# A two-layer attention encoder: x and the output on GpSimd's DMA queue, a norm weight spread by a one-row matmul, and a new order of the first work

## The chip, the core and the metric

The kernel runs on one core of a Trainium2 chip. The metric is the device time of one execution in microseconds (us). Five engines work side by side, each through its own list of instructions in order: TensorE (PE, with its weight loads as PEld), VectorE (DVE), ScalarE (ACT), GpSimd (POOL) and SyncE (SP), which only issues DMA transfers here. GpSimd can issue transfers too. Sixteen DMA engines carry them.

## What is computed

A sequence of 512 positions with 1024 features goes through two layers and a last norm. Cut to what matters:

```python
for l in range(2):
    h = rmsnorm(x, norm_g[l])
    proj = h @ w_in[l]                       # 1024 x 4096
    out_a = neighborhood_attention(...)      # 8 heads x 64, columns 0..2047 of proj
    out_b = diff_attention(...)              # 4 heads, two softmax maps each
    y = concat(out_a * silu(g_a), out_b * silu(g_b))
    x = x + y @ w_out[l]
return rmsnorm(x, final_g)
```

where `rmsnorm(x, g) = x * rsqrt(mean(x*x) + 1e-6) * g`.

## The kernel before, in words

The 512 rows of x are held as four tiles of 128 rows (t = 0 to 3), each loaded by two transfers of 64 rows (`x_load`, L428 to L432), on SyncE's queue. A matmul in full precision is made of three terms: each operand is split into a high part (fp32r) and the rest, and high x high, low x high and high x low are summed.

Weights come in units of 256 columns of `w_in`. `load_raw` (L79) loads half a unit (4 of 8 row chunks, 512 KB); a cast on ScalarE makes the high part `wh`, a subtraction on GpSimd or VectorE the low part `wl` (L99, L101). There are two raw buffers, so the next half is loaded when the low part of one is done.

The first unit's work (L450 to L503) is written out by hand, and `pinned` (L439) keeps each engine in the order in which the program was written. What stands there, in words:

- the first norm's 1024 weights are loaded as a 128 x 8 block `gcol` (L452) and spread over all partitions as `g_bc` by eight TensorE transposes and two copies (L465 to L469); `warm` fills TensorE with unneeded products ahead of and behind that;
- `norm_stat` (L215) squares and sums one tile of x on ScalarE (L218) and takes the inverse root on GpSimd (L210, L212); `norm_apply` (L221) scales the tile on VectorE (L228), transposes it on TensorE (L234) and splits it into `hTh` on ScalarE (L205) and `hTl` on VectorE (L206);
- the first unit (called w0 here, its halves w0-lo and w0-hi) is cast at L476 and L477; its low parts are made on GpSimd (L478) and VectorE (L480);
- for each tile t, `proj_tm` with `groups=True` (L257, L267) multiplies: 8 products hTh x wh, 8 hTl x wh, 8 hTh x wl. Then come the next tile's `norm_apply`, for t < 2 the second unit's casts (`conv1`), and the copy of the result (`vb0_evac`). The squares of tiles 2 and 3 stand in the program at t = 0.

After it, the position tables are written to memory by 16 transfers on SyncE's queue (`t5_skew`, L135), behind the two transfers that wrap `hTh` and `hTl` round (L239), which need the last tile. The rest of both layers is ordered by the framework's scheduler. At the end of the second layer (L586 to L604), each tile's last quarter is added, squared and summed; GpSimd makes the scale (L210, L212), ScalarE and VectorE scale the tile (L601, L602), and two transfers of 64 rows store it on SyncE's queue (L604).

## Time and profile before

| | |
|---|---|
| time of three runs | 631.53, 633.57, 634.60 us, median 633.57 |
| profiled execution, span from first to last instruction | 630.6 us, which is all that is known of its own time |
| TensorE busy | 591.7 us (94%), mean granted clock 0.981 |
| VectorE, ScalarE, GpSimd busy | 422.3, 324.6, 277.3 us |
| moved by DMA | 77.57 MB, 123 GB/s over the span |
| idle TensorE at the start (7.3 to 13.0 and 22.3 to 26.7 us) | 5.7 and 4.5 us |
| from the last product's end (619.5 us) to the end of the span | 11.1 us |

Busy times overlap between engines and do not add up to the span. A wait is shown in brackets behind the instruction that ended it, with what released it. In the rows that follow, a window's row gives the busy time of each engine in a stretch, the granted clock of TensorE (1.00 is 2.4 GHz), the mean busy share of the sixteen DMA engines, and the bytes per time that they moved.

### The profile page before, as it was taken

Reading aid. Unit: us, or ns where it says so; the run is one execution under the profiler, and the core shown is the slowest. Engines: PE = TensorE matmul, PEld = TensorE weight load, DVE = VectorE, ACT = ScalarE, POOL = GpSimd, SP = SyncE. Lnnn points to the kernel's source line nnn. Section 1 sums busy time; section 2 is a strip of 40 time slices with the busy share of each in tenths; the row PEclk is TensorE's granted clock in tenths of the full one; section 3 lists DMA queues with packets and bytes.
Section 4 is the critical chain, followed back from the end, with each engine's and each line's share of the span. In section 5 each row is a group of like instructions: output and inputs, shape, how many; then the busy total and the mean of one; then the engine's idle time right before and its main releaser. Section 6 shows DMA issues by size and latency. Waiting matters only on the chain.

```text
span 630.6 us, 10037 instructions
## 1 busy us (share of the span) xinstructions
PE 591.7 (94%) x3626; PEld 522.3 (83%) x3626; DVE 422.3 (67%) x907; ACT 324.6 (51%) x706; POOL 277.3 (44%) x232
## 2 busy tenths in 40 slices
PE   4799699999899999999999999999989999999992
PEld 3678597888799878889999898888879878889992
DVE  3552354997988868874564257798888968874542
ACT  3343353864766555744343455666567646654421
POOL 2341422444456747743143633344535665733111
PEclk9799899999999999999999999999999999999997
DMA  6566746552442454264454452342343444355204
GB/s 145 129 124 192 213 147 197 134 136 78 109 119 55 143 129 133 85 171 146 134 168 135 123 144 86 90 114 63 88 107 93 116 116 116 101 167 168 68 1 134
DMA packets 77448, 77.57 MB, mean 123 GB/s; under 512 B 9906, under 2 KB 71346, under 8 KB 76374
## 3 DMA queue, kind: packets, MB, share of 16 engines
q1 hardware_dynamic: 75926, 74.53, 41.7%
q0 software_dynamic: 1472, 2.40, 2.3%
q8 instruction: 29, 0.48, 0.3%
q14 instruction: 21, 0.17, 0.1%
HBM read 63.16 MB, written 9.37 MB: 115 GB/s over the span
## 4 chain that ended last, share of the span: by engine, by line
PE 58%; DMA 14%; DVE 10%; issue 5%; POOL 5%; SPq 5%; ACT 3%; POOLq 0%; ACTq 0%; DVEq 0%
PE pp L252 25%; PE pp L267 22%; DMA wraw<-in_w_in_dram 4%; DMA y<-in_x_dram 4%; SPq L135 3%; DVE ea L382 2%; POOL wl L101 2%; DMA yb_d<-tb_d 2%; POOL ba L179 2%; PE pv L338 2%; DVE kt L291 2%; DVE w4k L329 1%; PE pt L333 1%; PE st L316 1%; DMA rs_d<-rsb 1%
## 5 line engine op out<-in xcount | busy, mean ns | idle before, releaser
L101 POOL TENSOR_TENSOR wl<-wraw,wh 128x1024 fp32r<-128x1024 f32 x68 | 166.2, 2462 | 192.5 <-ACT wh L99 124.9
L99 ACT CAST wh<-wraw 128x1024 fp32r<-128x1024 f32 x78 | 78.8, 1046 | 72.2 <-DMA wraw<-in_w_in_dram 28.9
L252 PE MATMUL pp<-hTh,wh 128*128 128x512 f32 x384 | 103.4, 397 | 3.2 <-DVE kt L291 3.2
L252 PE MATMUL pp<-hTh,wl 128*128 128x512 f32 x384 | 106.3, 398 | 0.0
L252 PE MATMUL pp<-hTl,wh 128*128 128x512 f32 x384 | 104.5, 398 | 0.0
L252 PEld LDWEIGHTS pp<-hTh,wh 128*128 128x128 f32 x384 | 70.4, 188 | 17.7 <-issue 3.6
L252 PEld LDWEIGHTS pp<-hTh,wl 128*128 128x128 f32 x384 | 70.3, 189 | 14.5 <-issue 0.5
L252 PEld LDWEIGHTS pp<-hTl,wh 128*128 128x128 f32 x384 | 70.2, 188 | 13.9
L267 PE MATMUL pp<-wh,hTh 128*128 128x256 f32 x256 | 72.3, 302 | 7.7 <-ACT hTh L205 4.5
L267 PE MATMUL pp<-wh,yTh 128*128 128x256 f32 x256 | 72.4, 283 | 0.0
L267 PE MATMUL pp<-wl,yTh 128*128 128x256 f32 x256 | 72.3, 283 | 0.0
L267 PE MATMUL pp<-wh,yTl 128*128 128x256 f32 x256 | 71.9, 283 | 0.0
L267 PE MATMUL pp<-wh,hTl 128*128 128x256 f32 x256 | 70.3, 293 | 0.0
L206 DVE TENSOR_TENSOR ptl<-pt,pth 128x256 fp32r<-128x256 f32 (+1 forms) x96 | 48.2, 507 | 31.6 <-ACT pth L205 30.7
L267 PE MATMUL pp<-wl,hTh 128*128 128x256 f32 x256 | 68.9, 287 | 0.0
L205 ACT CAST pth<-pt 128x256 fp32r<-128x256 f32 (+1 forms) x96 | 42.0, 443 | 43.1 <-PE pt L333 29.3
L382 DVE TENSOR_SCALAR ea<-ea,rza 128x256 f32<-128x256 f32 x64 | 58.5, 914 | 1.8
L267 PEld LDWEIGHTS pp<-wh,hTh 128*128 128x128 f32 x256 | 49.3, 202 | 10.9 <-ACT hTh L205 5.0
L179 POOL TENSOR_TENSOR ba<-nmask,ya 128x256 f32<-128x256 f32 (+1 forms) x64 | 39.6, 650 | 32.3 <-DVE mna L376 18.5
L319 DVE CUSTOM_DVE_ANT_0 lt<-st,yb 128x512 f32<-128x512 f32 x64 | 43.5, 685 | 11.2 <-PE st L317 10.7
L267 PEld LDWEIGHTS pp<-wh,hTl 128*128 128x128 f32 x256 | 48.8, 199 | 0.8
L267 PEld LDWEIGHTS pp<-wh,yTh 128*128 128x128 f32 x256 | 49.1, 192 | 0.2
(111 smaller groups left out, 1141.0 us busy)
## 6 DMA issues: line engine op xcount, KB each, us to landing
wraw<-in_w_in_dram SPq DMA_DIRECT2D x32, 512.0 KB
wraw<-in_w_in_dram SPq DMA_DIRECT2D x64, 256.0 KB
kt<-kt SPq DMA_DIRECT2D x16, 512.0 KB
wraw<-in_w_out_dram SPq DMA_DIRECT2D x16, 512.0 KB
y<-in_x_dram SPq DMA_DIRECT2D x16, 256.0 KB
ya_d<-rp_d SPq DMA_DIRECT2D x32, 120.0 KB
ya<-ya_d SPq DMA_DIRECT2D x16, 240.0 KB
yb<-yb_d SPq DMA_DIRECT2D x8, 280.0 KB
```

Of the source, the lines that this page charges most:

```text
L99: A.copy(out=wh[:, ks, :], in_=r)
L101: eng.tensor_tensor(out=wl[:, ks, :], in0=r, in1=wh[:, ks, :].bitcast(F32), op=ALU.subtract)
L135: eng.dma_start(out=dst[:, i * C8:(i + 1) * C8, :], in_=bass.AP(tensor=src.tensor, offset=src.offset + base - step * r - C8 * b, ap=[[pitc ...
L179: G.tensor_tensor(out=ba[:, i0:i0 + n], in0=_view(nmask, i0 * C8, [[C8, n], [0, ROWS], [1, C8]]), in1=_view(y, w0, [[C8, n], [RPW, ROWS], ...
L205: A.copy(out=oh, in_=ps)
L206: V.tensor_tensor(out=ol, in0=ps, in1=oh.bitcast(F32), op=ALU.subtract)
L252: T.matmul(out=pp, lhsT=a[:, kc, cs], rhs=b[:, kc, c0:c0 + S], start=(n == 0), stop=(n == 3 * KC - 1))
L267: T.matmul(out=pp[:, 0:256], lhsT=a[kc][:, c0:c0 + P], rhs=b[:, kc, :], start=(n == 0), stop=(n == 3 * KC - 1))
L291: V.tensor_tensor(out=kl, in0=src, in1=kh.bitcast(F32), op=ALU.subtract)
L319: V.tensor_tensor_reduce(out=lt, in0=st, in1=yb[:, 48 - 16 * qt:560 - 16 * qt], scale=1.0, scalar=3e38, op0=ALU.add, op1=ALU.min, accum_ou ...
L338: T.matmul(out=pv[:, qp * 256:(qp + 1) * 256], lhsT=vt[:, kt, h % 2, vs, :], rhs=pp[:, kt, :], start=(n == 0), stop=(n == 11))
L382: V.tensor_scalar_mul(e, e, rz)
```

## The change

The loads of x at the start go to GpSimd's queue, and so do the stores of the output. The first norm's weights are loaded as one row of 1024, and a matmul of a row of 128 ones with it spreads the row over all partitions. In the hand-written part, the square of tile 1 now stands ahead of w0-hi's cast, and the squares of tiles 2 and 3 stand just ahead of their own tile's scaling. The 24 products of a tile are taken in another sequence: first the four row chunks of w0-lo with hTh and hTl, then those of w0-hi, then both with `wl`. Lines move down by two or three.

```diff
+    one_row = work.tile([1, P], F32, name="row", tag="th", bufs=2)
+    V.memset(one_row, 1.0)
...
         if groups:
-            seq = [(kc, terms[i]) for i in (0, 2, 1) for kc in order]
+            seq = [(kc, terms[i]) for h0, i in ((0, 0), (0, 2), (4, 0), (4, 2), (0, 1), (4, 1))
+                   for kc in range(h0, h0 + 4)]
...
-    def x_load(t):
+    def x_load(t, eng=nc.sync):
...
-            nc.sync.dma_start(out=xi[64 * i:64 * i + 64], in_=x_v[2 * t + i])
+            eng.dma_start(out=xi[64 * i:64 * i + 64], in_=x_v[2 * t + i])
...
-    gcol = const.tile([P, KC], F32, name="gcol")
-    nc.sync.dma_start(out=gcol, in_=norm_g[0].rearrange("(k p) -> p k", p=P))
-    xt = [x_load(0)]
+    g_row = w4.tile([1, D], F32, name="g_row", tag="w4k")
+    nc.sync.dma_start(out=g_row, in_=norm_g[0:1, :])
+    xt = [x_load(0, nc.gpsimd)]
     raws = [load_raw(W.seq[0], hf) for hf in range(2)]
-    xt += [x_load(t) for t in range(1, NB)]
+    xt += [x_load(t, nc.gpsimd) for t in range(1, NB)]
...
-        for j in range(4):
-            T.transpose(out=gp[:, j * P:(j + 1) * P], in_=_view(gcol, 4 * i + j, [[0, P]]), identity=ident)
+        T.matmul(out=gp, lhsT=one_row, rhs=g_row[:, i * S:(i + 1) * S], start=True, stop=True)
...
-    n0 = norm_stat(xt[0])
...
+    ns = [norm_stat(xt[0])]
     A.copy(out=w[0][:, lo, :], in_=raws[0])
+    G.tensor_tensor(out=w[1][:, lo, :], in0=raws[0], in1=w[0][:, lo, :].bitcast(F32), op=ALU.subtract)
+    norm_apply(0, xt[0], g_bc, *ns[0])
+    ns.append(norm_stat(xt[1]))
     A.copy(out=w[0][:, hi, :], in_=raws[1])
-    G.tensor_tensor(out=w[1][:, lo, :], in0=raws[0], in1=w[0][:, lo, :].bitcast(F32), op=ALU.subtract)
-    norm_apply(0, xt[0], g_bc, *n0)
...
-    ns = [n0, norm_stat(xt[1])]
     for t in range(NB):
         pp = proj_tm(w, 64 + t * P, kh, kl, groups=True)
-        if t == 0:
-            ns += [norm_stat(xt[2]), norm_stat(xt[3])]
         if t + 1 < NB:
+            if t:
+                ns.append(norm_stat(xt[t + 1]))
             norm_apply(t + 1, xt[t + 1], g_bc, *ns[t + 1])
...
-                            nc.sync.dma_start(out=out_v[2 * t + i], in_=xn[t][64 * i:64 * i + 64])
+                            nc.gpsimd.dma_start(out=out_v[2 * t + i], in_=xn[t][64 * i:64 * i + 64])
```

How the instructions then stand on the engines, at the three places of which the prediction speaks. First ScalarE in the hand-written start, before (y_113, y_120, y_123 and y_126 are tiles 0 to 3 of x, wraw_116 and wraw_118 the halves of w0, wraw_189 and wraw_192 those of the second unit):

```order
L218 ACTIVATE w4k_157,ss_158<-y_113 128x1024
L476 CAST wh_163<-wraw_116 128x1024
L477 CAST wh_163<-wraw_118 128x1024
L205 CAST hTh_129<-pt_170 128x4x128
L205 CAST hTh_129<-pt_177 128x4x128
L218 ACTIVATE w4k_197,ss_198<-y_120 128x1024
L218 ACTIVATE w4k_228,ss_229<-y_123 128x1024
L218 ACTIVATE w4k_234,ss_235<-y_126 128x1024
L205 CAST hTh_129<-pt_242 128x4x128
L205 CAST hTh_129<-pt_249 128x4x128
L99 CAST wh_195<-wraw_189 128x1024
L205 CAST v_185<-pp_203 128x2x128
```

And the same engine with the change (tiles 0 to 2 are y_115, y_122 and y_125, w0's halves wraw_118 and wraw_120, the second unit's first half wraw_191):

```order
L220 ACTIVATE w4k_155,ss_156<-y_115 128x1024
L478 CAST wh_153<-wraw_118 128x1024
L207 CAST hTh_131<-pt_165 128x4x128
L207 CAST hTh_131<-pt_172 128x4x128
L220 ACTIVATE w4k_179,ss_180<-y_122 128x1024
L482 CAST wh_153<-wraw_120 128x1024
L207 CAST hTh_131<-pt_226 128x4x128
L207 CAST hTh_131<-pt_233 128x4x128
L101 CAST wh_197<-wraw_191 128x1024
L207 CAST v_187<-pp_199 128x2x128
L220 ACTIVATE w4k_269,ss_270<-y_125 128x1024
L207 CAST hTh_131<-pt_277 128x4x128
```

The squares of tiles 2 and 3 stood ahead of tile 1's two `hTh` casts; now they stand behind the whole of the tile before. w0-hi's cast moved behind tile 1's square.

GpSimd in the same place, with the change (before, all four pairs L210 and L212 stood ahead of the two L101):

```order
L479 TENSOR_TENSOR wl_154<-wraw_118,wh_153 128x1024
L212 TENSOR_SCALAR ss_180<-ss_180 128x1
L214 TENSOR_TENSOR rs_183<-ss_180,nhalf_98 128x1
L103 TENSOR_TENSOR wl_198<-wraw_191,wh_197 128x1024
L212 TENSOR_SCALAR ss_270<-ss_270 128x1
L214 TENSOR_TENSOR rs_273<-ss_270,nhalf_98 128x1
L103 TENSOR_TENSOR wl_198<-wraw_194,wh_197 128x1024
L212 TENSOR_SCALAR ss_329<-ss_329 128x1
L214 TENSOR_TENSOR rs_332<-ss_329,nhalf_98 128x1
```

The scales of tiles 2 and 3 now each stand behind a low part of the second unit.

GpSimd at the end, with the change (xn_6308 holds tiles 0 and 1, xn_6309 tiles 2 and 3; the stores stood on SyncE before):

```order
L212 TENSOR_SCALAR ss_6695<-ss_6695 128x1
L214 TENSOR_TENSOR rs_6698<-ss_6695,nhalf_98 128x1
L606 DMA out_0_dram<-xn_6308 8x8x1024 x2
L212 TENSOR_SCALAR ss_6732<-ss_6732 128x1
L214 TENSOR_TENSOR rs_6735<-ss_6732,nhalf_98 128x1
L606 DMA out_0_dram<-xn_6308 8x8x1024 x2
L212 TENSOR_SCALAR ss_6769<-ss_6769 128x1
L214 TENSOR_TENSOR rs_6772<-ss_6769,nhalf_98 128x1
L212 TENSOR_SCALAR ss_6806<-ss_6806 128x1
L214 TENSOR_TENSOR rs_6809<-ss_6806,nhalf_98 128x1
L606 DMA out_0_dram<-xn_6309 8x8x1024 x4
```

The stores of tiles 2 and 3 stand together behind the last tile's scale.

## Rows read from the trace of the kernel before

**Rows 1.** The page: span, and the chain that ended last, by line.

```profile
span 630.6 us, 10037 instructions
...
PE pp L252 25%; PE pp L267 22%; DMA wraw<-in_w_in_dram 4%; DMA y<-in_x_dram 4%; SPq L135 3%; DVE ea L382 2%; POOL wl L101 2%; DMA yb_d<-tb_d 2%; POOL ba L179 2%; PE pv L338 2%; DVE kt L291 2%; DVE w4k L329 1%; PE pt L333 1%; PE st L316 1%; 
```

**Rows 2.** Windows at the start and one later; last come PEclk, DMA share, GB/s.

```profile
1.60:2.60 1.00, 1.00 (x5) 1.00 (x6) 0.00 (x0) 0.61 (x2) 0.00 (x0) 1.00 0.54 4
2.60:4.00 1.40, 1.40 (x8) 1.40 (x8) 0.00 (x0) 0.00 (x0) 0.00 (x0) 1.00 0.41 32
4.00:10.00 6.00, 3.32 (x21) 2.80 (x19) 1.38 (x2) 0.00 (x0) 0.00 (x0) 1.00 0.96 205
10.00:15.00 5.00, 1.11 (x4) 0.71 (x4) 2.81 (x2) 3.71 (x5) 3.50 (x3) 0.76 0.58 180
...
55.00:60.00 5.00, 5.00 (x23) 4.06 (x22) 0.54 (x1) 0.04 (x1) 0.00 (x0) 1.00 0.80 252
```

**Rows 3.** Timeline of ScalarE at the start: start us, us, instruction, idle before.

```profile
10.09 1.06 ACT L218 ACTIVATE w4k<-y 128x1024 f32<-128x1024 f32 x1 [7.87 <-DMA y<-in_x_dram]
...
11.14 1.03 ACT L476 CAST wh<-wraw 128x1024 fp32r<-128x1024 f32 x1
...
17.39 1.06 ACT L218 ACTIVATE w4k<-y 128x1024 f32<-128x1024 f32 x1
...
25.05 1.06 ACT L218 ACTIVATE w4k<-y 128x1024 f32<-128x1024 f32 x1 [3.07 <-DMA y<-in_x_dram]
...
26.11 1.05 ACT L205 CAST hTh<-pt 128x512 fp32r<-128x512 f32 x2
...
28.00 0.38 ACT L205 CAST v<-pp 128x256 fp32r<-128x256 f32 x1
```

**Rows 4.** Timelines of VectorE (first three) and GpSimd at the start.

```profile
12.19 3.51 DVE L228 SCALAR_TENSOR_TENSOR w4k<-y,rs,g_bc 128x512 f32<-128x512 f32 x2 [6.16 <-ACT wh L476]
...
18.14 1.22 DVE L480 TENSOR_TENSOR wl<-wraw,wh 128x1024 fp32r<-128x1024 f32 x1
20.08 1.42 DVE L228 SCALAR_TENSOR_TENSOR w4k<-y,rs,g_bc 128x512 f32<-128x512 f32 x2 [0.72 <-POOL rs L212]
...
12.25 2.91 POOL L478 TENSOR_TENSOR wl<-wraw,wh 128x1024 fp32r<-128x1024 f32 x1
...
28.18 2.38 POOL L101 TENSOR_TENSOR wl<-wraw,wh 128x1024 fp32r<-128x1024 f32 x1 [1.07 <-ACT wh L99]
```

**Rows 5.** Timeline of TensorE at the start.

```profile
16.53 2.25 PE L267 MATMUL pp<-wh,hTh 128*128 128x256 f32 x8
...
26.72 2.08 PE L267 MATMUL pp<-wh,hTh 128*128 128x256 f32 x8 [4.46 <-ACT hTh L205]
...
31.26 1.29 PE L234 MATMUL pt<-ident,w4k 128*128 128x128 f32 x8
...
38.58 0.75 PE L267 MATMUL pp<-wh,hTh 128*128 128x256 f32 x4
```

**Rows 6.** Windows at the end: columns as in rows 2.

```profile
615.30:620.00 4.70, 4.16 (x35) 3.95 (x33) 1.89 (x6) 1.79 (x5) 1.49 (x4) 1.00 0.51 150
...
625.00:629.30 4.30, 0.00 (x0) 0.00 (x0) 0.00 (x0) 0.00 (x0) 0.00 (x0) 0.50 0.44 142
629.30:630.60 1.30, 0.00 (x0) 0.00 (x0) 0.00 (x0) 0.00 (x0) 0.00 (x0) 0.50 0.00 0
```

**Rows 7.** Timeline of GpSimd at the end: its last scale.

```profile
621.35 0.55 POOL L212 TENSOR_TENSOR rs<-ss,nhalf 128x1 f32<-128x1 f32 x1
```

**Rows 8.** A 256 KB transfer on GpSimd's queue: its issue, two windows, all eight landings.

```profile
155.37 0.54 POOL L359 DMA_DIRECT2D rb<-rs_d  x1 [2.28 <-DMA rs_d<-rsb]
...
155.40:156.60 1.20, 1.20 (x9) 1.00 (x8) 0.00 (x0) 0.25 (x1) 0.51 (x1) 1.00 0.00 0
156.60:158.60 2.00, 2.00 (x12) 1.66 (x11) 1.18 (x2) 1.45 (x3) 0.00 (x0) 1.00 0.58 131
...
DMA to landing us min/median/max: 3.4/3.6/3.8
```

## The prediction

> **What bounds the kernel now.** I read the page's chain first: TensorE's two projection lines carry 47% of a span of 630.6 us, the loads of x 4% [rows 1]. The middle of the program keeps its order on every engine, so only the two ends can move: the first 39 us, where TensorE waits for data, and the last 15, where the output is stored. Whatever the start saves is handed on, since all that follows hangs on the fourth tile's product (38.58 [rows 5]). I take the ends apart by the windows and by each engine's timeline.
>
> *The start.* ScalarE waits 7.87 us for tile 0 of x, until 10.09 [rows 3]. From 1.6 to 2.6 the DMA engines are half busy with 4 GB/s, the 4-byte pieces of `gcol`; 32 GB/s follow until 4.0, then 205 at a share of 0.96 while x and w0 share one queue, then 180 at 0.58 once the loads of x are nearly alone [rows 2]. ScalarE's last wait for x, 3.07 us for tile 3, ends at 25.05; two casts of tile 1 stand behind it, and TensorE, idle for 4.46, starts tile 1's product at 26.72 [rows 3, 5].
>
> *The end.* From 615.3 to 629.3 the stores move 142 to 150 GB/s at a share of 0.44 to 0.51; 1.3 us without traffic close the span [rows 6]. So eight transfers of 256 KB are limited by their own rate, and half of the DMA engines stand idle all the while. The same mark, 0.58 at 180 GB/s, is on the loads of x.
>
> **The weight row.** Two matmuls of 512 columns and two copies replace eight transposes and the same copies, before tile 0 arrives. The cover is TensorE's wait for its first product at 16.53; without it they would cost some 2 us, the 2.25 of eight products at the lower clock level [rows 5]. I take 0. The removed `gcol` frees up to 1.0 us of the DMA engines ahead of x.
>
> **x on GpSimd's queue.** On that queue bytes follow the issue by 1.2 us, and 256 KB are there 3.4 to 3.8 after it [rows 8]. Tile 0 is issued behind two memsets, the other six transfers behind the identity, each issue 0.54, so all eight are out by 6 us, beside w0 on SyncE's queue. I let tile 0's bytes start at 2.4 (2.6 now, less a little for `gcol`), keep the slow 1.4 us (to 3.8), and add 1.0 for the landing (nearest row: the tail of 1.3 [rows 6]). The rate of both queues together lies between 205 and 252 GB/s [rows 2]; I take 225, nearer the row at the same place, with 130 for x and 95 for w0, an even split leaning to x's longer rows. Tile 0's 0.52 MB then take 4.0: it lands at **8.8**; w0-lo 5.5, at 10.3; w0-hi at 15.8; the last of x at 18.8. Bounds for tile 0: 205 halved, landing 9.9; nearly all of 252, landing 7.0.
>
> **The new order of the first work.** What follows tile 0 is counted from its landing, X.
>
> - Now the scaling of tile 1 (20.08) starts 10.0 behind X [rows 3, 4].
> - With the change, tile 0's scaling still runs against GpSimd's `wl` (3.51 for a pair that takes 1.42 alone, beside 2.91 of GpSimd [rows 4]), so `hTh` of tile 0 ends where it does now and tile 1's square follows at X + 7.4 (17.39 - 10.09 [rows 3]). Behind it now stand w0-hi's cast, 1.03 [rows 3], and `wl` of w0-hi on VectorE, 1.22 [rows 4], ahead of tile 1's scaling: 7.4 + 1.25 (the square, 1.06, with its read) + 1.03 + 1.22 and hand-overs = **X + 11.0**. The new order costs 1.0 here: that cast lay in ScalarE's idle time.
> - From tile 1's scaling to tile 3's product it is 38.58 - 20.08 = 18.5 now [rows 4, 5], with the 3.07 wait inside. The change removes that wait, but the squares of tiles 2 and 3 come late. Counted from tile 1's scaling: tile 0's product ends at 2.6 (16 of its 24 products wait for w0-hi's cast); transposes, 1.29 [rows 5], and two casts end at 5.0, a weight cast at 6.0, the copy of v, 0.38, and tile 2's square at 7.7. GpSimd first makes 2.38 of `wl` [rows 4], until 8.4, then two small steps (0.55 for the larger [rows 7]) until 9.1; scaling, transposes and casts until 11.8. Then weight cast, tables (taken like a cast), v and square, 1.03 + 1.03 + 0.38 + 1.25, until 15.5; small steps until 16.3; half a scaling, 0.7, half the transposes, 0.65, and one cast, 0.6, until 18.3. I take 18.6 with hand-overs: the order puts back the wait that it removed.
>
> Start: 10.1 + 10.0 + 18.5 = 38.6 now; then 8.8 + 11.0 + 18.6 = 38.4, a gain of **0.2**. Its sign hangs on X (zero at 9.0): X = 9.9 loses 0.9, X = 7.0 gains 2.0.
>
> **The stores on GpSimd's queue.** GpSimd's scale for tile 3 ends at 621.9 [rows 7]; behind it stand the four stores of tiles 2 and 3, 0.54 each [rows 8], out by 624.1. Tile 2's, which go out before that scale now, wait for it. First bytes at 621.9 + 1.2 = 623.1. These 1.05 MB are bounded from both sides: at 150 GB/s 7.0 us (end of traffic 630.1), at 300, both halves of a tile on different DMA engines, 3.5 (626.6). I take 3.9 (627.0), near the fast end, since a share of 0.51 [rows 6] leaves eight engines idle and another queue's transfers need not go to the busy eight. With the tail of 1.3: 628.3 for 630.6, a gain of **2.3**. Bounds: gain 2.7, loss 0.8. Tile 1's stores also slip, by a square; they are out before tile 2's and cost nothing.
>
> *A rule against it.* The Trainium skill's DMA: Bandwidth & Descriptors, section Issuing engines are not separate DMA queues, says that transfers run on the same sixteen engines whoever issues them, and that spreading them over issuers saves issue time only. By it the end would lose the 0.8; the share of 0.51 in rows 6 shows engines that the stores leave unused, which that reading does not foresee.
>
> **Sum.** 0.2 + 2.3 = 2.5 of the profiled 630.6 gives 628.1; the median of the runs lies 2.97 above that span, so 633.57 - 2.5 = **631.1**.
>
> **Rivals.**
>
> 1. *The stores stay at half rate* (chance 0.2). GpSimd's transfers go to the same eight engines, or its queue moves no more than the 131 GB/s of rows 8 (then 8.0 us, 1.0 more). For it: that row. Against it: that transfer reads one 2 KB row 128 times, unlike a store. The end loses 0.8 instead of gaining 2.3: 633.57 - 0.2 + 0.8 = 634.2.
> 2. *x crowds out w0: slower* (chance 0.22). If each DMA engine takes turns by rows, 4 KB of x against 1 KB of w0, then w0-lo's 0.52 MB are through only with all 2.1 MB of x: at the 205 of rows 2, 3.8 + 12.8 + 1.0 = 17.6. Cast, two casts of `hTh`, square, w0-hi's cast and its `wl` (1.03 + 1.05 + 1.25 + 1.03 + 1.22 = 5.6) put tile 1's scaling at 23.2, 3.1 later than now, and tile 3's product 3.2 later. With the end's 2.3: 633.57 + 3.2 - 2.3 = 634.5; with rival 1's end 637.6. It decides where w0-lo lands after 14.4, or w0-hi after 17.5. For it: x is issued on a queue of its own and no longer waits its turn behind w0. Against it: w0 now goes out as SyncE's second and third transfers, ahead of most of x.
> 3. *Both loads fit* (chance 0.16). At 252 GB/s tile 0 comes nearly alone, at 7.0, and w0 still in time (both 3.15 MB are through by 17.3): start 2.0, end 2.7, so 628.9.
>
> **How the numbers follow.** My case has 0.42. The range takes in the rivals' 628.9 and 634.5 and the spread of three runs, 1.5 either way: 627.8 to 636.0. A measurement of this kernel tells about 0.5%, 3.2 us, from no change. Faster than 630.4: rival 3 and the better part of my case (0.16 + 0.2), 0.36. Slower than 636.7: rivals 1 and 2 together, 0.07. Between: 0.57.
>
> **What would show it.** Tile 0: its square starts near 8.8, and the DMA share of the first 15 us stays near 1. Order: tile 1's scaling comes 11 behind the first square's start, ScalarE waits for no later tile of x, GpSimd's small steps stand right behind a `wl`, and tile 3's product starts at 38.4. Stores: a share near 1 and 250 to 300 GB/s from 623 to 627, and nothing behind 627. Wrong it would be with a share of 0.5 there (rival 1); with w0-lo's cast waiting for its load past 14 (rival 2); with tile 3's product before 36.6 (rival 3); or with any change over 1 us between 40 and 610 us, which I take to be the same work in the same order.

## The result and the profile after

The change makes the kernel slower. Its median is 642.59 us (639.76 to 645.06, four executions) against 634.09 for the kernel before on the same chip (631.53 to 636.05): a ratio of 1.015, 95% interval 1.0113 to 1.0188. The forecast was 631.1 in a range of 627.8 to 636.0.

The profiled execution has a span of 643.2 and took 645.06, 1.9 above its span. By the same 1.9 the profiled execution of before, with its span of 630.6, stands for some 632.5 (an estimate). So these two executions lie 12.6 apart, more than the medians (8.5): the profiled one of after is its slowest, that of before lies below its median.

The page of after: span, and the chain that ended last by engine and by line.

```profile
span 643.2 us, 10036 instructions
...
PE 57%; DVE 13%; DMA 11%; issue 5%; POOL 5%; SPq 4%; ACT 4%; POOLq 0%; ACTq 0%; DVEq 0%
PE pp L270 25%; PE pp L254 20%; DMA wraw<-in_w_in_dram 4%; SPq L137 3%; POOL wl L103 3%; DVE w4k L332 2%; PE pv L341 2%; DVE ea L385 2%; PE st L373 2%; DMA wraw<-in_w_out_dram 2%; DVE lt L322 2%; PE pt L388 1%; DMA y<-in_x_dram 1%; DMA kt<-kt 1%; PE pt L336 1%
```

The loads of x fall from 4% of the chain [rows 1] to 1%, as they should. But GpSimd's low parts (L103) and VectorE's L332 have moved up: L332 combines the two softmax maps of a head in attention B, in the first layer's middle, which the change does not touch.

Where the 12.6 us come from is read by taking instructions that stand in the same place in both kernels and subtracting their starts:

| instruction | before | after | later by |
|---|---|---|---|
| tile 3's first product (L267, now L270) | 38.58 [rows 5] | 43.01 | 4.4 |
| first product of a map with v (L338, now L341) | 110.39 | 115.02 | 4.6 |
| the combination of two maps (L329, now L332) | 124.83 | 130.10 | 5.3 |
| VectorE's next instruction (L319, now L322) | 125.50 | 135.67 | 10.2 |
| GpSimd's last scale (L212, now L214) | 621.35 [rows 7] | 633.26 | 11.9 |
| end of the span | 630.6 | 643.2 | 12.6 |

Two jumps stand out: the start, and one instruction at 130 us. Between the first two rows, though, TensorE's lag does not stand still: a product at 87.76 before (L316) starts at 89.95 after, 2.2 later, and the lag stays there until the product of the second row. The timeline of before, SyncE and then TensorE, at that place:

```profile
100.65 0.94 SPq L84 DMA_DIRECT2D wraw<-in_w_in_dram  x2
...
110.39 0.39 PE L338 MATMUL pv<-pth,v 128*128 128x256 f32 x1 [1.39 <-ACT pth L205]
```

And the timeline of after, SyncE, ScalarE and TensorE:

```profile
105.80 0.94 SPq L86 DMA_DIRECT2D wraw<-in_w_in_dram  x2
...
112.22 1.04 ACT L101 CAST wh<-wraw 128x1024 fp32r<-128x1024 f32 x1 [8.22 <-DMA wraw<-in_w_in_dram]
...
115.02 0.58 PE L341 MATMUL pv<-pth,v 128*128 128x256 f32 x1 [3.82 <-ACT pth L207]
```

The product waits for the cast of `pth`, which stands on ScalarE behind two weight casts; these wait for loads that SyncE issues behind sixteen transfers of the position tables, 5.2 us later than before. So here the lateness comes back to TensorE by way of SyncE's list.

These are the windows of after: busy time of each engine, then granted clock, DMA share and GB/s.

```profile
4.00:10.00 6.00, 6.00 (x15) 3.23 (x14) 1.38 (x2) 0.00 (x0) 2.49 (x7) 1.00 1.12 241
10.00:15.00 5.00, 3.25 (x15) 2.55 (x13) 2.22 (x2) 2.34 (x4) 2.92 (x3) 1.00 1.06 220
28.80:31.10 2.30, 0.01 (x1) 0.00 (x0) 0.86 (x2) 0.00 (x0) 1.24 (x3) 1.00 0.17 49
31.10:41.60 10.50, 10.45 (x36) 6.74 (x37) 3.78 (x6) 4.59 (x8) 5.45 (x8) 0.52 0.36 95
111.00:115.00 4.00, 0.20 (x1) 0.00 (x0) 0.00 (x0) 2.60 (x4) 1.66 (x1) 0.82 0.51 182
115.00:120.00 5.00, 4.98 (x18) 4.50 (x19) 4.91 (x11) 4.54 (x11) 5.00 (x6) 0.50 0.61 157
126.00:131.00 5.00, 5.00 (x28) 4.10 (x27) 4.41 (x10) 5.00 (x11) 1.08 (x2) 1.00 0.09 33
131.00:136.00 5.00, 2.98 (x24) 2.71 (x23) 5.00 (x2) 0.26 (x1) 5.00 (x3) 1.00 0.38 105
136.00:141.00 5.00, 5.00 (x26) 4.59 (x26) 4.73 (x13) 1.99 (x4) 1.77 (x3) 0.66 0.27 55
...
634.00:638.00 4.00, 0.00 (x0) 0.00 (x0) 0.40 (x1) 0.46 (x1) 2.16 (x4) 0.72 0.58 154
638.00:639.50 1.50, 0.00 (x0) 0.00 (x0) 0.00 (x0) 0.00 (x0) 0.00 (x0) 0.50 0.82 292
639.50:643.20 3.70, 0.00 (x0) 0.00 (x0) 0.00 (x0) 0.00 (x0) 0.00 (x0) 0.50 0.01 1
```

**The start.** x does come faster: the DMA engines are busy without a break (share 1.12 and 1.06, 241 and 220 GB/s, for 0.96 and 0.58, 205 and 180 GB/s, before [rows 2]). Yet TensorE does nothing from 28.8 to 31.1, and for the next 10.5 us its granted clock is 0.52, nearly all at the lower level of 1.2 GHz. The timeline of after (start, us, instruction, idle before it), first the start, by engine:

```profile
10.67 1.06 ACT L220 ACTIVATE w4k<-y 128x1024 f32<-128x1024 f32 x1 [8.45 <-DMA y<-in_x_dram]
...
37.17 1.05 ACT L220 ACTIVATE w4k<-y 128x1024 f32<-128x1024 f32 x1
...
21.23 1.41 DVE L230 SCALAR_TENSOR_TENSOR w4k<-y,rs,g_bc 128x512 f32<-128x512 f32 x2
...
30.24 1.42 DVE L230 SCALAR_TENSOR_TENSOR w4k<-y,rs,g_bc 128x512 f32<-128x512 f32 x2 [2.68 <-POOL rs L214]
...
39.26 1.42 DVE L230 SCALAR_TENSOR_TENSOR w4k<-y,rs,g_bc 128x512 f32<-128x512 f32 x2 [1.54 <-POOL rs L214]
...
26.92 2.39 POOL L103 TENSOR_TENSOR wl<-wraw,wh 128x1024 fp32r<-128x1024 f32 x1 [6.88 <-ACT wh L101]
...
31.14 1.75 PE L236 MATMUL pt<-ident,w4k 128*128 128x128 f32 x8 [2.33 <-DVE w4k L230]
32.82 3.57 PE L153 MATMUL st<-oh,t5s 32*4 32x512 f32 x4
...
43.01 0.73 PE L270 MATMUL pp<-wh,hTh 128*128 128x256 f32 x4 [0.24 <-ACT hTh L207]
```

The waits are a chain: the square of tile 2 stands late on ScalarE, GpSimd makes a low part first (26.92 to 29.31), so VectorE's scaling of tile 2 waits 2.68 for GpSimd's scale, and TensorE 2.33 for that scaling. The same square-scale-scaling chain holds tile 3 (square at 37.17, scaling at 39.26). Behind the idle stretch the eight transposes take 1.75 us; before, they took 1.29 [rows 5].

**The middle.** The timeline of before, VectorE and then GpSimd around the combination:

```profile
124.83 0.75 DVE L329 SCALAR_TENSOR_TENSOR w4k<-w4k,rz 128x512 f32<-128x512 f32 x1
125.50 0.68 DVE L319 CUSTOM_DVE_ANT_0 lt<-st,yb 128x512 f32<-128x512 f32 x1
...
124.63 0.56 POOL L353 DMA_DIRECT2D ms<-row  x1 [8.82 <-DVE row L351]
125.21 5.00 POOL L101 TENSOR_TENSOR wl<-wraw,wh 128x1024 fp32r<-128x1024 f32 x2
```

The same place in the timeline of after:

```profile
130.10 5.65 DVE L332 SCALAR_TENSOR_TENSOR w4k<-w4k,rz 128x512 f32<-128x512 f32 x1
135.67 0.68 DVE L322 CUSTOM_DVE_ANT_0 lt<-st,yb 128x512 f32<-128x512 f32 x1
...
129.89 0.56 POOL L356 DMA_DIRECT2D ms<-row  x1 [9.45 <-DVE row L354]
130.47 4.71 POOL L103 TENSOR_TENSOR wl<-wraw,wh 128x1024 fp32r<-128x1024 f32 x2
```

One instruction of VectorE takes 5.65 us instead of 0.75: it lies over GpSimd's whole pair of low parts and ends half a microsecond behind it. TensorE, fed by VectorE here, is busy for 2.98 of 5 us from 131 to 136, and its clock is 0.66 in the next five. This pair of low parts belongs to the eighth weight unit; I call the event the **lock-out**.

**The end.** The last transfers move 292 GB/s at a share of 0.82, for 150 at 0.51 before [rows 6]; but 3.7 us almost without traffic follow, where before there were 1.3 [rows 6].

### The profile page after: what moved, and what is told of

It reads as the page before. It is cut to its first block, busy times and chain, and to the rows that moved or that the text cites. A ratio compares the mean times of both kernels' runs of the same rounds, so it can differ in the third digit from the quotient of the medians.

```text
span 643.2 us, 10036 instructions
## 1 busy us (share of the span) xinstructions
PE 603.6 (94%) x3622; PEld 529.9 (82%) x3622; DVE 424.3 (66%) x908; ACT 324.5 (50%) x706; POOL 286.2 (44%) x248
## 4 chain that ended last, share of the span: by engine, by line
PE 57%; DVE 13%; DMA 11%; issue 5%; POOL 5%; SPq 4%; ACT 4%; POOLq 0%; ACTq 0%; DVEq 0%
PE pp L270 25%; PE pp L254 20%; DMA wraw<-in_w_in_dram 4%; SPq L137 3%; POOL wl L103 3%; DVE w4k L332 2%; PE pv L341 2%; DVE ea L385 2%; PE st L373 2%; DMA wraw<-in_w_out_dram 2%; DVE lt L322 2%; PE pt L388 1%; DMA y<-in_x_dram 1%; DMA kt<-kt 1%; PE pt L336 1%
## 5 line engine op out<-in xcount | busy, mean ns | idle before, releaser
L103 POOL TENSOR_TENSOR wl<-wraw,wh 128x1024 fp32r<-128x1024 f32 x68 | 165.9, 2456 | 200.6 <-ACT wh L101 123.1
L101 ACT CAST wh<-wraw 128x1024 fp32r<-128x1024 f32 x78 | 78.7, 1046 | 72.9 <-DMA wraw<-in_w_in_dram 27.7
L270 PE MATMUL pp<-wh,hTh 128*128 128x256 f32 x256 | 73.5, 304 | 3.4 <-DVE kt L294 2.0
L270 PE MATMUL pp<-wh,yTh 128*128 128x256 f32 x256 | 72.4, 283 | 0.6 <-ACT yTh L207 0.6
L270 PE MATMUL pp<-wl,yTh 128*128 128x256 f32 x256 | 72.3, 283 | 0.0
L270 PE MATMUL pp<-wh,hTl 128*128 128x256 f32 x256 | 72.2, 299 | 0.0
L270 PE MATMUL pp<-wh,yTl 128*128 128x256 f32 x256 | 71.9, 283 | 0.0
L270 PE MATMUL pp<-wl,hTh 128*128 128x256 f32 x256 | 71.1, 298 | 0.0
L270 PEld LDWEIGHTS pp<-wh,hTh 128*128 128x128 f32 x256 | 50.0, 204 | 7.6 <-issue 4.4
L270 PEld LDWEIGHTS pp<-wh,hTl 128*128 128x128 f32 x256 | 50.1, 204 | 1.0 <-DVE hTl L208 0.2
L325 ACT ACTIVATE w4k<-lt,mn 128x512 f32<-128x512 f32 x64 | 46.0, 722 | 9.4 <-DVE mn L322 9.0
L322 DVE CUSTOM_DVE_ANT_0 lt<-st,yb 128x512 f32<-128x512 f32 x64 | 43.4, 684 | 11.1 <-PE st L320 9.9
## 6 DMA issues: line engine op xcount, KB each, us to landing
y<-in_x_dram POOLq DMA_DIRECT2D x8, 256.0 KB, 10.6
```

The costliest lines, as they stand in the source:

```text
L101: A.copy(out=wh[:, ks, :], in_=r)
L103: eng.tensor_tensor(out=wl[:, ks, :], in0=r, in1=wh[:, ks, :].bitcast(F32), op=ALU.subtract)
L270: T.matmul(out=pp[:, 0:256], lhsT=a[kc][:, c0:c0 + P], rhs=b[:, kc, :], start=(n == 0), stop=(n == 3 * KC - 1))
L322: V.tensor_tensor_reduce(out=lt, in0=st, in1=yb[:, 48 - 16 * qt:560 - 16 * qt], scale=1.0, scalar=3e38, op0=ALU.add, op1=ALU.min, accum_ou ...
L325: A.activation(out=e[:, m, :].rearrange("p (b r c) -> p b r c", r=ROWS, c=C8), in_=lt.rearrange("p (r b c) -> p b r c", r=ROWS, c=C8), fun ...
```

## The experiments

Each kernel was run beside the kernel before on the same chip. The table gathers what the text below reads from them: the ratio to before with its 95% interval, and from the one profiled execution of each the start of tile 3's first product, the start and length of the combination of two maps (all in us), and the time from that start to the end of the span.

| kernel | ratio | tile 3's product | combination | takes | from there to the end |
|---|---|---|---|---|---|
| before | 1 | 38.58 | 124.83 | 0.75 | 505.8 |
| after | 1.015 (1.0113 to 1.0188) | 43.01 | 130.10 | **5.65** | 513.1 |
| e1, x alone | 1.0038 (1.0019 to 1.0057) | 35.92 | 122.46 | **5.63** | 511.4 |
| e2, order alone | 1.0044 (1.0026 to 1.0062) | 41.96 | 126.35 | 0.75 | 509.0 |
| e3, stores alone | 1.0004 (0.9982 to 1.0026) | 39.76 | 123.55 | 0.75 | 510.0 |
| e12, row alone | 1.0064 (1.0039 to 1.0089) | 39.76 | 126.48 | 0.75 | 511.2 |
| e4, tile 3 delayed | 1.0003 (0.9987 to 1.002) | 42.34 | 123.73 | 0.75 | 509.7 |
| e5, x on ScalarE's queue | 0.9992 (0.9966 to 1.0017) | 38.15 | 124.12 | 0.75 | 506.9 |
| e6, e1 with a spacer | 1.0034 (1.0011 to 1.0058) | 35.03 | 119.77 | **5.66** | 510.4 |
| e7, eight tiny loads | 1.0151 (1.0115 to 1.0187) | 40.85 | 129.87 | **5.66** | 513.2 |
| e16, sixteen memsets | 1.0157 (1.0118 to 1.0195) | 42.37 | 128.38 | **5.63** | 514.1 |
| e10, e1 with a hold | **0.994** (0.9911 to 0.9969) | 35.15 | 120.88 | 0.75 | 508.3 |
| e9, after with a hold | 1.0083 (1.0053 to 1.0113) | 42.99 | 127.44 | 0.75 | 508.9 |
| e8, after, early squares | 1.0087 (1.0055 to 1.0118) | 36.54 | 121.62 | **5.64** | 513.9 |
| e13, after, block not row | 1.0107 (1.0071 to 1.0142) | 42.35 | 127.14 | **5.64** | 512.1 |
| e11, after, x on ScalarE's queue | 1.0141 (1.0111 to 1.017) | 43.28 | 128.09 | 0.75 | 513.1 |
| e14, e10 with the row | 0.9966 (0.9936 to 0.9997) | 35.33 | 124.64 | 0.75 | 508.4 |
| e15, all three mended | 0.9991 (0.9961 to 1.0021) | 35.45 | 120.32 | 0.75 | 508.3 |

### One part at a time

x alone on GpSimd's queue, from the kernel before:

```diff
-    def x_load(t):
+    def x_load(t, eng=nc.sync):
...
-            nc.sync.dma_start(out=xi[64 * i:64 * i + 64], in_=x_v[2 * t + i])
+            eng.dma_start(out=xi[64 * i:64 * i + 64], in_=x_v[2 * t + i])
...
-    xt = [x_load(0)]
+    xt = [x_load(0, nc.gpsimd)]
...
-    xt += [x_load(t) for t in range(1, NB)]
+    xt += [x_load(t, nc.gpsimd) for t in range(1, NB)]
```

> The kernel before with only the loads of x moved to GpSimd's queue. Theory (the new order of squares and low parts costs the start, and chance meetings of VectorE with GpSimd cost the middle): tile 0 lands near 10.7 as in the changed kernel, but ScalarE's 3.07 us wait for tile 3 goes; tile 3's product at 36.5 to 38.5 (38.58 before), time 630 to 635. Rival (x on the other queue is itself the loss): tile 3's product at 41 or later, time 640 or more.

Measured: 636.44 for 634.63, slower by 0.38%. The theory's range ended at 635. The start gains 2.7 us (35.92), and ScalarE no longer waits for any tile of x behind the first. But the combination takes 5.63 and gives it all back, and more.

The new order alone (the squares, casts and the sequence of products, as in the change's diff):

```diff
-            seq = [(kc, terms[i]) for i in (0, 2, 1) for kc in order]
+            seq = [(kc, terms[i]) for h0, i in ((0, 0), (0, 2), (4, 0), (4, 2), (0, 1), (4, 1))
+                   for kc in range(h0, h0 + 4)]
...
+    ns.append(norm_stat(xt[1]))
+    A.copy(out=w[0][:, hi, :], in_=raws[1])
...
-        if t == 0:
-            ns += [norm_stat(xt[2]), norm_stat(xt[3])]
         if t + 1 < NB:
+            if t:
+                ns.append(norm_stat(xt[t + 1]))
```

> The kernel before with only the new order of squares, casts and products. Theory: the squares of tiles 2 and 3 behind the second unit's casts and low parts put tile 3's product at 41 to 44 (38.58 before), TensorE's granted clock falls to 0.5 behind its wait near 30, and the time is 638 to 645. Rival (the order is harmless, x's queue does it): product at 38 to 39.5, time 633 to 636.

Measured: 637.21 for 634.63, slower by 0.44% and just under the theory's 638, with tile 3's product 3.4 us later and no lock-out. From 31.1 to 41.6 us TensorE's granted clock is 0.58.

The stores alone:

```diff
-                            nc.sync.dma_start(out=out_v[2 * t + i], in_=xn[t][64 * i:64 * i + 64])
+                            nc.gpsimd.dma_start(out=out_v[2 * t + i], in_=xn[t][64 * i:64 * i + 64])
```

> The kernel before with only the stores of the output on GpSimd's queue. What the changed kernel's trace says: from the last product's end to the end of the span 12.0 (11.1 before), so 0.9 slower, time 634 to 636. Rival (the prediction): 8.8, so 2.3 faster, time 631.8.

Measured: 634.42 for 634.63, no difference. Windows of this kernel at its end, columns as above:

```profile
624.00:628.00 4.00, 0.00 (x0) 0.00 (x0) 0.55 (x1) 0.61 (x1) 2.67 (x5) 0.59 0.51 138
628.00:630.20 2.20, 0.00 (x0) 0.00 (x0) 0.00 (x0) 0.00 (x0) 0.00 (x0) 0.50 0.78 261
630.20:633.50 3.30, 0.00 (x0) 0.00 (x0) 0.00 (x0) 0.00 (x0) 0.00 (x0) 0.50 0.02 9
```

The faster traffic is there (261 GB/s), and so is the quiet tail, 3.3 us for 1.3 [rows 6]. The one pays for the other.

The weight row alone:

```diff
+    one_row = work.tile([1, P], F32, name="row", tag="th", bufs=2)
+    V.memset(one_row, 1.0)
...
-    gcol = const.tile([P, KC], F32, name="gcol")
-    nc.sync.dma_start(out=gcol, in_=norm_g[0].rearrange("(k p) -> p k", p=P))
+    g_row = w4.tile([1, D], F32, name="g_row", tag="w4k")
+    nc.sync.dma_start(out=g_row, in_=norm_g[0:1, :])
...
-        for j in range(4):
-            T.transpose(out=gp[:, j * P:(j + 1) * P], in_=_view(gcol, 4 * i + j, [[0, P]]), identity=ident)
+        T.matmul(out=gp, lhsT=one_row, rhs=g_row[:, i * S:(i + 1) * S], start=True, stop=True)
```

> The kernel before with only the weight row and its two one-row matmuls in place of the block and eight transposes. The prediction: nothing, within 0.5 of before. Rival (the matmuls at the lower clock, 3.8 us for four passes, push what follows): tile 0's scaling later and up to 2 slower.

Measured: 637.34 for 633.76, slower by 0.64%. Tile 3's product is 1.2 us later, which it is in e3 too, and the profiled execution takes 511.2 from the combination to the end, where the other kernels without lock-out take 505.8 to 510.0, and e11 513.1. The single parts lose 0.38 + 0.44 + 0.04 + 0.64 = 1.5%, which is what the whole loses. That the sum fits does not show that the parts add up: the part for x holds a gain and a lock-out, and in the changed kernel the order and the row are worth other amounts (e8 and e13 below).

### Is a late start what costs?

Three unneeded copies of tile 3 on ScalarE, ahead of its `hTh` casts, in the kernel before:

```diff
+        if g_bc is not None and t == NB - 1:
+            for i in range(3):
+                A.activation(out=xt, in_=xt, func=AF.Copy)
```

> The kernel before with three unneeded copies of tile 3 on ScalarE (1.06 us each) ahead of tile 3's casts; all else keeps its order. Tile 3's product near 41.8, 3.2 later. Theory (the middle's loss hangs on when VectorE's and GpSimd's work meet, not on what was changed): the lag does not stay at 3.2 but moves by 2 us or more, up or down, between 100 and 150 us, with VectorE instructions over 2 us beside a low part of GpSimd. Rival (a late start is handed on one for one): lag 3.2 all through, time 637.3, within 1.

Measured: 635.16 for 634.63, no difference, though tile 3's product starts at 42.34, 3.8 us later than before. The combination comes at 123.73, 1.1 earlier than before, and takes 0.75: the theory missed too, since the lag is gone without any such meeting. Where it goes, the timeline of TensorE shows. In before:

```profile
75.24 0.55 PE L267 MATMUL pp<-wh,hTh 128*128 128x256 f32 x1 [3.23 <-DVE kt L291]
```

And in e4:

```profile
75.79 0.36 PE L270 MATMUL pp<-wh,hTh 128*128 128x256 f32 x1 [0.64 <-DVE kt L294]
```

From 60 to 80 us TensorE of before waits for other work three times, 5.9 us in all, and that of e4 only here. SyncE's list, too, has caught up: it issues the weight loads of the result section at 100.71, for 100.65 before. So a late fourth product alone costs nothing: my step "whatever the start saves is handed on" is false as a rule.

The changed kernel with the squares of tiles 2 and 3 early again:

```diff
+        if t == 0:
+            ns += [norm_stat(xt[2]), norm_stat(xt[3])]
         if t + 1 < NB:
-            if t:
-                ns.append(norm_stat(xt[t + 1]))
```

> The changed kernel with the squares of tiles 2 and 3 back where they were before (ahead of tile 1's casts, their small steps ahead of the second unit's low parts). Theory (the late squares cost the start): tile 3's product at 38 to 40 instead of 43.0, no half clock between 31 and 41, time 3 to 4.5 below the changed kernel's 642.6: 638 to 639.5. Rival (the start's loss is swallowed later, as the 3.2 us of the delay were): within 1 of 642.6.

Measured: 638.1 for 632.57, a ratio of 1.0087 for the 1.015 of the changed kernel: the late squares cost some 0.6%, 4 us (the two intervals touch at their ends). Windows of this kernel over the two stretches in which the changed one stood idle and then ran slowly:

```profile
28.80:31.10 2.30, 1.86 (x10) 1.00 (x11) 1.53 (x3) 1.16 (x3) 0.00 (x0) 1.00 0.58 173
31.10:41.60 10.50, 10.45 (x66) 8.35 (x65) 4.87 (x8) 3.62 (x9) 7.82 (x11) 1.00 0.61 104
```

In both kernels TensorE is busy for 10.45 of the second stretch's 10.50 us: with the squares late it gets through 36 instructions at a clock of 0.52, with them early through 66 at 1.00. "Busy" hides this; the clock column and the counts show it. But the slow clock alone does not explain why this costs 4 us in the end and e4's late product nothing: e4, too, has a wait and a clock of 0.59 behind it, from 40 to 48 us, and its loss is taken up later. That the late squares cost is shown; which part of that the idle stretch, the slow clock and the lateness on SyncE's list have is open, since no run changes one of them alone.

### What makes the combination wait

Two explanations stood for the lock-out: transfers on GpSimd's queue, or the mere timing of GpSimd's list. x on ScalarE's queue, in the kernel before (x as in e1, with `nc.scalar`):

```diff
-    xt = [x_load(0)]
+    xt = [x_load(0, nc.scalar)]
...
-    xt += [x_load(t) for t in range(1, NB)]
+    xt += [x_load(t, nc.scalar) for t in range(1, NB)]
```

> The kernel before with the loads of x on ScalarE's queue instead of SyncE's; GpSimd's list of instructions stays as before. Theory (x on GpSimd's queue cost 4.8 us only because of one VectorE instruction that GpSimd's low parts locked out for 5.6 us near 122, and that hangs on GpSimd's own list): tile 3's product 2 to 3 earlier than before, no VectorE instruction over 5 us between 115 and 140, the lag stays near -2.6, time 631 to 633. Rival (x early on any second queue shifts the middle into that lock-out): lag turns from -2.6 to +2 near 128, time 636.5.

Measured: 632.21 for 632.57, no difference, no lock-out; tile 3's product gains 0.4, not the 2 to 3 of the theory. From 10 to 15 us the DMA share is 0.54 at 144 GB/s, near that of SyncE's queue (0.58 at 180 [rows 2]), where with x on GpSimd's queue it reaches 1.06 at 227 (e1) in the same window.

e1 with a short memset on GpSimd behind the issue of `ms`, to move the low parts a little:

```diff
         rs = small.tile([P, 4], F32, name="rsb")
+        issue = nc.cur_bb.bb.instructions[-1].name
+        G.memset(rs, 0.0)
+        behind(nc.cur_bb.bb.instructions[-1], issue)
```

> As the first experiment (x on GpSimd's queue), with one GpSimd memset of a 128x4 tile put between the DMA issue of ms and what follows it, in all eight attention heads of that kind. Theory: the low part comes a little later than VectorE's combination of the two maps, so VectorE goes first, takes 0.75 us instead of 5.63, and TensorE does not idle near 123 to 129; time 631.5 to 633.5. Rival (what GpSimd issues there makes no difference): the 5.6 us instruction stays and so does 636.4.

Measured: the combination still takes 5.66 us, 634.2 for 632.57. This run missed: the spacer delays nothing, since GpSimd goes on to the low parts right behind it (120.12 and 0.12 us long, low parts at 120.18).

Eight loads of 4 bytes on GpSimd's queue at the head of the kernel before, which nothing needs, and then sixteen memsets of 32 bytes on GpSimd instead, with no transfer at all:

```diff
+    dum = const.tile([1, 8], F32, name="dum")
+    for i in range(8):
+        nc.gpsimd.dma_start(out=dum[:, i:i + 1], in_=norm_g[0:1, i:i + 1])
```

> The kernel before with eight unneeded loads of 4 bytes on GpSimd's queue at the start, where the changed kernel has its eight loads of x; x stays on SyncE's queue. Theory (GpSimd's longer list of instructions is enough): the 5.6 us VectorE instruction appears near 125, the lag to before grows by 4 to 5 there, time 638 to 640. Rival (the data of x in flight, or its arrival, is needed): no such instruction, time 634 to 635.

```diff
+    dum = const.tile([1, 8], F32, name="dum")
+    for i in range(16):
+        G.memset(dum, 0.0)
```

> The kernel before with sixteen unneeded memsets of 32 bytes at the head of GpSimd's list; no transfer is added or moved. Theory (the mere number of instructions ahead decides which of the two engines comes first near 124): the packet of the instruction queue that now lies 1.1 us behind GpSimd's first ms comes earlier, VectorE's instruction takes 5.6 us, the lag grows by 4 to 5 there, time 637 to 640. Rival (it takes transfers on GpSimd's queue): packet and instruction as before, 633 to 635.

Measured: 643.12 for 632.57 (1.0151) and 644.32 for 634.61 (1.0157), both above the 640 at which the theories ended, and both with the lock-out at the same place, 120 us behind the added work. The timeline of VectorE in e7:

```profile
129.87 5.66 DVE L329 SCALAR_TENSOR_TENSOR w4k<-w4k,rz 128x512 f32<-128x512 f32 x1
```

And in e16:

```profile
128.38 5.63 DVE L329 SCALAR_TENSOR_TENSOR w4k<-w4k,rz 128x512 f32<-128x512 f32 x1
```

So neither x nor its transfers bring it about: a few more instructions on GpSimd's list suffice. The 1.5%, though, is not the price of the lock-out alone. Both kernels also start later, by 2.3 and 3.8 us, since the last tile of x lands later (ScalarE starts on it at 27.27 and 27.92, for 25.05 [rows 3]), and the combination itself starts 5.0 and 3.6 later. Why x lands later there, on the same queue as before, is open. The lock-out is in the seven kernels whose list on GpSimd is longer than before ahead of the combination and which have no hold, and in none of the others.

What the list's length does: the recorded starts are the same to 0.01 us in both kinds, counted from the `row` instruction ahead (123.68 before, 128.94 after): `ms` 0.95 behind it, the combination 1.16, the low parts 1.53. But in the trace itself GpSimd's two semaphore instructions ahead of the first low part stand 0.36 us earlier in after (1.00 and 1.12 us behind `row`, for 1.36 and 1.48), and by 0.3 to 0.4 us so in all seven kernels with the lock-out. And an instruction queue differs, q14, which I take for GpSimd's, since its packets move with GpSimd's list and not with another's. The DMA view of before, 124 to 127 us, by queue:

```profile
q0 software_dynamic: 32, 0.00, 4.7%
q14 instruction: 1, 0.01, 0.8%
```

The same view of after, 129 to 132 us:

```profile
q0 software_dynamic: 32, 0.00, 3.2%
```

Before, GpSimd fetches a block of its instructions just here, 1.1 us behind the issue of `ms`; so do the other kernels with the same list on GpSimd up to there (e2 to e5, e11 and e12). With a longer list the fetch comes earlier (in after between 112 and 116 us), and GpSimd is not held. That the fetch is the brake is inferred from where it lies, and not closely: its packet starts 2.03 us behind `row`, behind the delay, so that at most the request for it can have held GpSimd. That a longer list sets the lock-out off is shown, by three ways of making it longer.

The Trainium skill's SBUF — State Buffer, section Who interferes with whom, says that VectorE and GpSimd share one pair of ports under an exclusive lock, that a VectorE instruction with two inputs from SBUF contends with a GpSimd instruction that reads SBUF, and that the order of issue decides who blocks. The combination has two such inputs, and the 5.65 beside 0.75 us agree. By the recorded starts, though, the combination is 0.37 us ahead of the low parts in both kinds; these starts do not show who takes the ports first. The trace goes further: VectorE waits through two GpSimd instructions back to back. It does not always. In the timeline of before, the same instruction of VectorE, and then GpSimd, for another head:

```profile
160.85 2.96 DVE L329 SCALAR_TENSOR_TENSOR w4k<-w4k,rz 128x512 f32<-128x512 f32 x1
...
160.85 5.21 POOL L101 TENSOR_TENSOR wl<-wraw,wh 128x1024 fp32r<-128x1024 f32 x2 [0.61 <-ACT wh L99]
```

Here it waits for the first low part and comes in ahead of the end of the second. So such waits stand in the kernel before as well; the change adds a long one. The Trainium skill's Runtime: NRT & Kernel Launch, section Instruction fetch mechanics, calls the cost of passing from one block of instructions to the next mostly hidden; if the inference above holds, 0.36 us of it decides over 4.9 here.

A hold settles it. The two low parts of the eighth unit are made to wait for the combination, in e1 and then in the changed kernel:

```diff
+    mix = []
...
             eng.tensor_tensor(out=wl[:, ks, :], in0=r, in1=wh[:, ks, :].bitcast(F32), op=ALU.subtract)
+            if n == 7:
+                tc.add_manual_dep(nc.cur_bb.bb.instructions[-1], mix[7],
+                                  mybir.DependencyInfo(mybir.DependencyClass.Sync,
+                                                       mybir.DependencyReason.DATA), reason="order")
...
                                        op0=ALU.mult, op1=ALU.add)
+                mix.append(nc.cur_bb.bb.instructions[-1].name)
```

> The first experiment (only x on GpSimd's queue) with the same wait. Theory: the gain of the start, 2.7 to 3.5, is kept: lag to before about -3 from 30 us to the end, time 630.5 to 632 where before has 634. Rival (another meeting takes the place of this one): 635 or more.

> The changed kernel with one wait more: GpSimd's two low parts of the eighth unit (the pair that held VectorE up for 5.65 us at 130.1) wait for that VectorE instruction. Theory: VectorE's instruction takes 0.75 again, the pair starts 0.4 later, TensorE does not idle there and keeps its clock; time 4 to 6 lower than the changed kernel, 637 to 639. Rival (what VectorE loses there is caught up later): 641 to 643.

Measured: e10 631.05 for 633.76, a ratio of 0.994 (0.9911 to 0.9969), where e1 had 1.0038: the hold is worth about 1%. It is the fastest kernel of this study and beats both. e9 638.28 for 633.76: 1.0083 for 1.015, worth 0.7%, or 4.3 us. VectorE and GpSimd in e10:

```profile
120.88 0.75 DVE L334 SCALAR_TENSOR_TENSOR w4k<-w4k,rz 128x512 f32<-128x512 f32 x1
...
121.87 4.75 POOL L102 TENSOR_TENSOR wl<-wraw,wh 128x1024 fp32r<-128x1024 f32 x2 [0.63 <-PE st L322]
```

The low parts start 0.6 us later behind `ms` than in e1, and the time shows no price for it. The table's last column says the same for the kernels without a hold: the seven with the lock-out need 512.6 us on average from the combination to the end, the seven others 509.4.

### What is left of the loss

The changed kernel with x on ScalarE's queue, which also removes the lock-out:

```diff
-    xt = [x_load(0, nc.gpsimd)]
+    xt = [x_load(0, nc.scalar)]
...
-    xt += [x_load(t, nc.gpsimd) for t in range(1, NB)]
+    xt += [x_load(t, nc.scalar) for t in range(1, NB)]
```

> The changed kernel with x on ScalarE's queue, so that GpSimd's list has no loads at its head, as before; order, weight row and stores stay as changed. Theory (GpSimd's longer list makes the 5.6 us meeting): no VectorE instruction over 5 us between 115 and 140; the order's loss at the start stays; time 636 to 639. Rival (the data's queue does not matter): 5.6 us instruction present, 641 to 644.

Measured: 643.04 for 633.76, a ratio of 1.0141, no better than the changed kernel. The expectation missed: the lock-out is gone (0.75), but the start is as late (43.28), and from the combination to the end it needs 513.1, some 4 more than its kind. In the timeline of TensorE in e11, one wait stands out:

```profile
229.59 1.22 PE L373 MATMUL st<-kt,qs 128*128 128x256 f32 x4 [2.58 <-DMA kt<-kt]
```

Before, TensorE waits 0.3 us for that transfer; around it the lag of e11 grows by 3.7. What delays the transfer is open.

The changed kernel with the block and the transposes in place of the row, and e10 with the row:

```diff
-    g_row = w4.tile([1, D], F32, name="g_row", tag="w4k")
-    nc.sync.dma_start(out=g_row, in_=norm_g[0:1, :])
+    gcol = const.tile([P, KC], F32, name="gcol")
+    nc.sync.dma_start(out=gcol, in_=norm_g[0].rearrange("(k p) -> p k", p=P))
...
-        T.matmul(out=gp, lhsT=one_row, rhs=g_row[:, i * S:(i + 1) * S], start=True, stop=True)
+        for j in range(4):
+            T.transpose(out=gp[:, j * P:(j + 1) * P], in_=_view(gcol, 4 * i + j, [[0, P]]), identity=ident)
```

> The changed kernel with the weights as the 128 x 8 block and eight transposes again; order, x and stores as changed. If the weight row costs what it cost alone (0.64% of before, 4 us): 638.5 to 639.5. Rival (the row alone only met a chance that is not there in the changed kernel): 641.5 to 644.

```diff
-    gcol = const.tile([P, KC], F32, name="gcol")
-    nc.sync.dma_start(out=gcol, in_=norm_g[0].rearrange("(k p) -> p k", p=P))
+    g_row = w4.tile([1, D], F32, name="g_row", tag="w4k")
+    nc.sync.dma_start(out=g_row, in_=norm_g[0:1, :])
...
-        for j in range(4):
-            T.transpose(out=gp[:, j * P:(j + 1) * P], in_=_view(gcol, 4 * i + j, [[0, P]]), identity=ident)
+        T.matmul(out=gp, lhsT=one_row, rhs=g_row[:, i * S:(i + 1) * S], start=True, stop=True)
```

> The tenth experiment (x on GpSimd's queue, low parts held) with the weight row added. If the row costs by itself: 3 to 4.5 over the tenth, about 635, level with before. Rival: within 1 of the tenth, 630 to 632.

Measured: e13 640.99 for 633.82 (1.0107 for 1.015), e14 631.68 for 633.82 (0.9966 for 0.994). e13 lies between its two expectations, e14 with its rival, within 1 of the tenth. So the row costs 0.64% alone (e12), 0.43% in the changed kernel and 0.26% on e10, with intervals that overlap in the last two. That it costs is shown only where it stands alone; for the others some 2 us are an estimate from these ratios. By which path is open, since tile 3's product moves by only 0.2 to 1.2 us in these pairs.

Last, the changed kernel with all three mended: block, early squares, hold. What stays of the change is x and the stores on GpSimd's queue, tile 1's square ahead of w0-hi's cast, and the new sequence of products.

```diff
-        T.matmul(out=gp, lhsT=one_row, rhs=g_row[:, i * S:(i + 1) * S], start=True, stop=True)
+        for j in range(4):
+            T.transpose(out=gp[:, j * P:(j + 1) * P], in_=_view(gcol, 4 * i + j, [[0, P]]), identity=ident)
...
+            if n == 7:
+                tc.add_manual_dep(nc.cur_bb.bb.instructions[-1], mix[7],
...
+        if t == 0:
+            ns += [norm_stat(xt[2]), norm_stat(xt[3])]
...
-            if t:
-                ns.append(norm_stat(xt[t + 1]))
```

> The changed kernel without its three losses: the block of weights, the squares of tiles 2 and 3 early, the eighth unit's low parts held; x and stores on GpSimd's queue, the new sequence of products and tile 1's square ahead of w0-hi's cast stay. Theory (these three are all of the loss): as the tenth experiment or a little better, 629 to 632, ratio to before 0.992 to 0.997. Rival (the sequence of products or the stores cost too): 633 or more.

Measured: 633.96 for 633.82, a ratio of 0.9991: the whole loss is gone, but the theory missed; time and ratio are the rival's. Taken singly, the three are worth 0.67% (e9), 0.63% (e8) and 0.43% (e13), 1.73% together, and all at once 1.59%. That e15 does not reach the 0.994 of e10 leaves 0.5% for the stores, the sequence of products and tile 1's square, or for chance, as the intervals overlap: open.

## Why the prediction was wrong

**The middle, taken as unchanged.** This is the step that failed most. "The middle of the program keeps its order on every engine, so only the two ends can move" is true of the order and wrong of the time: the lock-out costs 4.9 us on VectorE and 0.7 to 1.0% of the time (e9, e10). The profile of before held a warning that I did not read: its combination of 0.75 us ends 0.37 behind the recorded start of a 5.00 us pair of GpSimd's. Of the 7.3 us that the stretch from the combination to the end adds between the profiled executions, 4.9 are this instruction; the other 2.4, with 0.9 of the stores in them, are no effect of the change that the runs show, since kernels without lock-out, too, need 509.0 us on average from there, where the profiled execution of before needs 505.8.

**Tile 0's landing (8.8).** It was 10.67, beyond my late bound (9.9) and even later than before (10.09). Both queues together moved 241 GB/s, more than the 225 that I took. So the rate was right or better and the split was off: w0-lo was there by 11.72, where its cast starts without a wait. Rival 2's extreme, w0 held back to 14.4, did not occur, and e1 shows what x on this queue is worth at the start: 2.7 us, more than I gave it, because the last tiles no longer make ScalarE wait.

**From tile 0 to tile 1's scaling (11.0).** Measured 21.23 - 10.67 = 10.6: right.

**From tile 1's scaling to tile 3's product (18.6).** Measured 43.01 - 21.23 = 21.8. Tile 2's scaling came 9.0 behind tile 1's (9.1 forecast): the chain through GpSimd's low part is right. What follows was mis-sized: 9.0 to tile 3's scaling where I had 7.2, and 3.75 to its product where I had 2.0. I took transposes, tables and products at the full clock, and did not ask what TensorE's idle time does to it: the granted clock is 0.52 from 31.1 to 41.6, and e8, with no idle stretch there, has 1.00. The order costs 3.4 us at tile 3's product alone (e2) and 0.6% in the changed kernel (e8); I had it put back only the wait that x gave.

**What the start is worth.** I passed it on one to one, through the fourth tile's product on which "all that follows hangs". That path was wrong. The product at 110 us follows the weight loads that SyncE issues behind its transfers of the tables, by 8.2 to 9.7 us in all eighteen profiled executions (110.39 behind 100.65 before, 115.02 behind 105.80 after). e4, with its fourth product 3.8 late, has these loads at 100.71 and loses nothing. e2 and e8 say that the late squares' loss stays.

**The weight row (0).** It loses 0.64% alone (e12), and 0.43 and 0.26% by ratios whose intervals overlap (e13, e14). The cover that I named is there in the profile of after (TensorE still waits 1.45 ahead of its first transposes), so the cover held. That the row would do nothing beyond it was the error; what it does, and by which path, is open.

**The stores (a gain of 2.3).** The traffic term was right in kind: 250 GB/s and more, where the forecast had 3.9 us for 1.05 MB. The tail was not: I carried over 1.3 us from SyncE's queue, and it is 3.3 to 3.7 on GpSimd's. From the last product's end to the end of the span it is 12.0 us for 11.1, a loss of 0.9 in the profiled pair, and nothing in the time of e3. The rule that I weighed (the Trainium skill's DMA: Bandwidth & Descriptors, Issuing engines are not separate DMA queues) gave a loss of 0.8, near the outcome; but the share of 0.82 and 292 GB/s speak against its reason, since the transfers of the other queue found DMA time that SyncE's stores leave idle (a share is a mean over the sixteen engines, and no view shows which of them stood idle). Rival 1 is wrong for the same reason; that its 0.8 is near the outcome is luck.

**The offset.** 2.97 us between profiled span and median were taken as fixed. The time of an execution lies 1.7 to 1.9 above its own span in these runs; the rest was that the profiled execution of before was a quick one.

**The chances.** 0.07 for slower was what two rivals at once would give, both at the ends. No case had the things that the runs found: an idle stretch with a slow clock behind it in the first 42 us, a list of SyncE's that hands lateness on, and one engine's instruction shutting out another's.
